# Feed-forward of a transformer layer by Strassen's products of halves, with the hidden activations and the sum in DRAM

## The chip, the cores and the metric

The kernel runs on one core of one Trainium2 chip. The metric is the device time of one execution in microseconds (us); the number that stands for a kernel is the median of several runs. Engines: PE multiplies matrices, DVE (VectorE), ACT (ScalarE) and POOL (GpSimd) work on elements, SP only issues transfers. "PEld" is PE's loading of the stationary operand.

## The reference

One layer of an encoder on x of 512 tokens by 2048 features, in float32: three sub-layers, each `x <- x + RMSNorm(sublayer(RMSNorm(x)))`. The first two (token mixers, cross-attention) are not touched. The third is a dense SwiGLU feed-forward with D_FF = 5632:

```python
def swiglu_ffn(h, w_gu, w_down):
    gate, up = jnp.split(h @ w_gu, 2, axis=-1)     # (512, 2048) @ (2048, 11264)
    return (jax.nn.silu(gate) * up) @ w_down       # (512, 5632) @ (5632, 2048)

x = x + rmsnorm(swiglu_ffn(rmsnorm(x, g[FFN_PRE]), ffn_w_gu[l], ffn_w_down[l]), g[FFN_POST])
```

## The kernel before, in words

Every float32 matrix `a` is split into two float32r tiles, `hi` (ACT casts, L145 or L148) and `lo = a - hi` (DVE, L146 or L149), and a product of two such matrices is three matmuls, hi by hi, hi by lo and lo by hi (`mul3`, L163 to L166). So one instruction of PE takes a stationary block of 128 by 128 and streams 256 or 512 columns past it, and every weight that comes from DRAM costs ACT and DVE one operation each before PE can use it.

Phase 1 (mixers) and phase 2 (cross-attention) run up to about 1403 us. Phase 2 ends with `y_proj`: it leaves y in SBUF, and `advance` (L742 on), for two token tiles of 128 at a time, adds the normed y to the residual stream (L752, in place in the tile `ad_x`), writes that to DRAM (`x2_d`, by a DMA from POOL, L754; the trace calls it `x_d`), transposes it on PE (L218) and splits it into the operand `act`, which is neither normed nor multiplied by the gain: the gain is a scale in the split of the weights (L148, L149), and the norm's factor is multiplied in when the products leave PSUM (`rB`, L928, L931).

Phase 3 is the feed-forward. `gu(b)` makes 512 of the 5632 hidden features by `proj_a`: weights of 128 features by 128 columns are stationary and the tokens stream, 512 columns per matmul; for b = 0 this is done in two halves of 256 tokens, the first of which needs only the first two token tiles. The silu is tanh on ACT (L929) and three operations on DVE (L928 to L931), the product with the up half is L935, and the result is split into `ff_h`, `ff_l` in SBUF. `down(b)` multiplies these 512 features by `proj_b`: the tokens (`ff_h`) are stationary and 512 columns of `w_down` stream; DVE adds the result to y in SBUF (L953). The loop is `gu(0)`, then `gu(b)`, `down(b-1)` for b = 1 to 10, then `last(10)`, which takes one token tile after the other through the last 512 hidden features and the final norm to the output (L981 adds, L983 sums squares, L989 multiplies by the gain, L995 adds the residual).

A scheduler sets each engine's order ahead of time; the engines then run their lists in that order and wait for each other by semaphores. SP issues the loads, in its own order too.

Of the kernel before, what the change touches and what calls it, by code (L numbers as in the profile page):

```python
# [15 lines left out]
P = 128  # L16
# [14 lines left out]
# columns of w_in  # L31
# [4 lines left out]
# columns of the constant tile  # L36
# [3 lines left out]
# columns of the parameter tiles  # L40
# [21 lines left out]
def build(tc, x, mem, norm_g, w_in, conv_a_w, pool_w, pool_scale, gdn_conv_w, gdn_A_log,  # L62
          gdn_dt_bias, gdn_norm_g, ssm_conv_w, ssm_conv_b, ssm_A_log, ssm_dt_bias, ssm_D,
          ssm_norm_g, w_out, xa_wq, xa_wkv, xa_wo, ffn_w_gu, ffn_w_down, cst, out, dbg=None,
# [9 lines left out]
    cp = pool("cp")  # L74
    wp = pool("wp", 3)
    ap_ = pool("actp", 8)
    sm = pool("smp", 4)
    mm = pool("mm", 5, space=PSUM)
    ps = pool("ps", 3, space=PSUM)
# [4 lines left out]
    w_gu, w_down, pool_w = ffn_w_gu[0], ffn_w_down[0], pool_w[0]  # L84
# [9 lines left out]
    r2f = cp.tile([P, NT], F32, name="r2f")  # L94
# [8 lines left out]
    x2_d = dr.tile([T, D], F32, name="x2_d")  # L103
    z_d = dr.tile([T, 512], F32, name="z_d")
# [37 lines left out]
    def split(hi, lo, src, scale=None):  # L142
        """hi + lo = src (times a per-partition scale), each in float32r's bits."""
# [19 lines left out]
    def mul3(o, ah, al, bh, bl, start, stop):  # L163
        nc.tensor.matmul(o, ah, bh, start=start, stop=False)  # L164
        nc.tensor.matmul(o, ah, bl, start=False, stop=False)  # L165
        nc.tensor.matmul(o, al, bh, start=False, stop=stop)  # L166
# [17 lines left out]
    def proj_b(lhs, nk, W, r0, c0, evict, tiles, gain=None, pre=None, done=None):  # L184
        """Token-major: 512 columns of W by the tokens of each tile; lhs(k, t) -> (hi, lo)."""
# [45 lines left out]
    def norm_rows(src, pl):  # L231
        """1 / rms of a token tile [128, 2048], as a column."""
# [37 lines left out]
    def kv_proj(mt, c0, dst, pl, pre=None, done=None):  # L270
        """Keys (or values) of a head, feature-major and split, to DRAM."""
# [60 lines left out]
    def gate_weights(gp):  # L332
        """The sixteen columns of w_in that make the rates, split."""
# [28 lines left out]
    def gates(o, nh, bias, a_log, gp, tg):  # L362
        """Rates and decays of a recurrence's heads, token-major; column nh * t + head."""
# [10 lines left out]
        # softplus(u) = max(u, 0) + log1p(e), e = exp(-|u|); log1p(e) = 2 artanh(e / (2 + e))  # L374
# [662 lines left out]
```

## Time and profile before

| | us |
|---|---|
| median of 3 runs (lowest, highest) | 2879.02 (2877.52, 2879.63) |
| span of the profiled execution, first to last instruction | 2875.84 |
| what lies around the span, median less span | 3.2 |
| phases 1 and 2, to the last matmul of `y_proj` | 1403.5 |
| feed-forward up to the last matmul of `down` | 1416.3 |
| `last(10)`, to the end of the span | 56.0 |

PE is busy for 99% of the span. "Busy" says that a matmul was under way, not that PE went at its peak: the matmuls overlap (a matmul of 512 columns is listed with 0.39 us, the next starts 0.23 us later), so the rate is read from start to start in the timeline, or as a count over a stretch.

### The profile page before, as it was taken

How to read it: one execution, taken by the hardware profiler on the slowest of the kernel's cores; microseconds unless marked ns; L12 is line 12 of the kernel's file. 1: busy time of each engine (PE TensorE's matmuls, PEld its weight loads, DVE VectorE, ACT ScalarE, POOL GpSimd, SP SyncE). 2: the span in 40 equal slices, each digit the busy share in tenths (PEclk: the TensorE clock that was granted, in tenths of full speed). 3: DMA queues.
4: the chain of work that ended last, by engine and by line, in shares of the span. 5: the costliest groups of instructions: out<-in, count | busy, mean ns of one | idle time of the engine just before them, and what ended most of it. 6: DMA issues, size and time to landing. Idle time of an engine off the chain costs nothing.

```text
span 2875.8 us, 34036 instructions
## 1 busy us (share of the span) xinstructions
PE 2836.4 (99%) x13354; PEld 2344.7 (82%) x13354; DVE 1408.4 (49%) x2509; ACT 994.1 (35%) x1648; POOL 84.7 (3%) x135
## 2 busy tenths in 40 slices
PE   8999999999999999999999999999999999999998
PEld 6788788888788878888898888888888888888886
DVE  5736556455842374334963443434444434434446
ACT  5623432333542264334652222222222222222222
POOL 0000000000000010000000000000000000000002
PEclk9999999999999999999999999999999999999999
DMA  8633222344682285424762233233323223332323
GB/s 279 233 103 96 84 74 72 118 132 163 211 319 98 95 311 207 141 88 168 260 195 96 95 96 97 98 99 96 95 95 95 95 95 96 98 98 98 96 98 144
DMA packets 179308, 382.92 MB, mean 133 GB/s; under 512 B 17214, under 2 KB 18123, under 8 KB 173899
## 3 DMA queue, kind: packets, MB, share of 16 engines
q1 hardware_dynamic: 169994, 342.98, 36.4%
q0 software_dynamic: 9152, 37.75, 3.5%
q8 instruction: 105, 1.72, 0.2%
q14 instruction: 57, 0.46, 0.0%
HBM read 338.72 MB, written 41.97 MB: 132 GB/s over the span
## 4 chain that ended last, share of the span: by engine, by line
PE 90%; DVE 4%; issue 2%; DMA 2%; ACT 2%; POOL 0%; SPq 0%; DVEq 0%; ACTq 0%; POOLq 0%
PE mm L164 28%; PE mm L166 28%; PE mm L165 28%; DVE wlo L149 1%; PE ps L520 1%; PE ps L524 1%; DMA raw<-in_xa_wkv_dram 1%; PE ps L218 1%; DVE ad_x L995 0%; DMA memt<-in_mem_dram 0%; ACT gd_jk L430 0%; PE ps L164 0%; ACT whi L148 0%; DVE rsq_t L138 0%; DMA xt<-in_x_dram 0%
## 5 line engine op out<-in xcount | busy, mean ns | idle before, releaser
L149 DVE SCALAR_TENSOR_TENSOR wlo<-raw,PA,whi 128x512 fp32r<-128x512 f32 x752 | 536.2, 747 | 811.2 <-ACT whi L148 807.8
L164 PE MATMUL mm<-act,whi 128*128 128x512 f32 (+1 forms) x2368 | 900.4, 380 | 0.0
L166 PE MATMUL mm<-act,wlo 128*128 128x512 f32 (+1 forms) x2368 | 897.2, 379 | 0.0
L165 PE MATMUL mm<-act,whi 128*128 128x512 f32 (+1 forms) x2368 | 897.1, 379 | 0.0
L148 ACT ACTIVATE whi<-raw,PA 128x512 fp32r<-128x512 f32 x752 | 505.2, 718 | 1023.0 <-PE mm L165 689.8
L166 PEld LDWEIGHTS mm<-act,wlo 128*128 128x128 f32 x2368 | 445.7, 188 | 81.9 <-issue 0.5
L164 PEld LDWEIGHTS mm<-act,whi 128*128 128x128 f32 x2368 | 445.8, 188 | 80.9 <-issue 0.7
L165 PEld LDWEIGHTS mm<-act,whi 128*128 128x128 f32 x2368 | 445.9, 188 | 80.7 <-issue 0.7
L146 DVE TENSOR_TENSOR wlo<-raw,whi 128x1024 fp32r<-128x1024 f32 x172 | 210.5, 1224 | 405.0 <-ACT whi L145 404.8
L145 ACT CAST whi<-raw 128x1024 fp32r<-128x1024 f32 x172 | 180.8, 1052 | 490.7 <-PE mm L166 323.0
L164 PE MATMUL mm<-whi,act 128*128 128x512 f32 x640 | 252.8, 396 | 3.3 <-ACT act L145 3.3
L165 PE MATMUL mm<-wlo,act 128*128 128x512 f32 x640 | 251.9, 394 | 1.8 <-DVE wlo L149 1.8
L164 PE MATMUL mm<-whi,ff_h 128*128 128x512 f32 x640 | 252.6, 395 | 0.0
L166 PE MATMUL mm<-whi,ff_l 128*128 128x512 f32 x640 | 252.5, 395 | 0.0
L165 PE MATMUL mm<-wlo,ff_h 128*128 128x512 f32 x640 | 252.5, 395 | 0.0
L166 PE MATMUL mm<-whi,act 128*128 128x512 f32 x640 | 251.0, 393 | 0.2 <-DVE act L146 0.2
L164 PEld LDWEIGHTS mm<-whi,act 128*128 128x128 f32 x640 | 120.9, 189 | 30.3 <-ACT act L145 5.4
L165 PEld LDWEIGHTS mm<-wlo,act 128*128 128x128 f32 x640 | 121.1, 189 | 27.7 <-DVE wlo L149 3.0
L166 PEld LDWEIGHTS mm<-whi,ff_l 128*128 128x128 f32 x640 | 120.6, 188 | 28.2
L165 PEld LDWEIGHTS mm<-wlo,ff_h 128*128 128x128 f32 x640 | 120.6, 188 | 28.1
L164 PEld LDWEIGHTS mm<-whi,ff_h 128*128 128x128 f32 x640 | 120.6, 188 | 28.1
L166 PEld LDWEIGHTS mm<-whi,act 128*128 128x128 f32 x640 | 121.0, 189 | 25.3 <-DVE act L146 0.6
(363 smaller groups left out, 2179.1 us busy)
## 6 DMA issues: line engine op xcount, KB each, us to landing
raw<-in_ffn_w_gu_dram SPq DMA_DIRECT2D x192, 512.0 KB, 3.4
raw<-in_w_in_dram SPq DMA_DIRECT2D x88, 512.0 KB, 3.5
raw<-in_ffn_w_down_dram SPq DMA_DIRECT2D x88, 512.0 KB, 3.9
raw<-in_xa_wkv_dram SPq DMA_DIRECT2D x64, 512.0 KB, 4.4
raw<-in_w_out_dram SPq DMA_DIRECT2D x32, 512.0 KB, 3.9
raw<-in_xa_wo_dram SPq DMA_DIRECT2D x32, 512.0 KB, 6.2
raw<-in_xa_wq_dram SPq DMA_DIRECT2D x32, 512.0 KB, 4.0
raw<-vw_d SPq DMA_DIRECT2D x28, 512.0 KB, 4.1
```

What stands on the lines that cost most here:

```text
L145: nc.scalar.copy(hi, src)
L146: nc.vector.tensor_tensor(lo, src, hi.bitcast(F32), op=ALU.subtract)
L148: nc.scalar.activation(hi, src, AF.Copy, scale=scale)
L149: nc.vector.scalar_tensor_tensor(lo, src, scale, hi.bitcast(F32), op0=ALU.mult, op1=ALU.subtract)
L164: nc.tensor.matmul(o, ah, bh, start=start, stop=False)
L165: nc.tensor.matmul(o, ah, bl, start=False, stop=False)
L166: nc.tensor.matmul(o, al, bh, start=False, stop=stop)
L218: nc.tensor.transpose(tp[:, j], src[:, k * P:(k + 1) * P], ident)
L520: nc.tensor.matmul(h64(tp)[:, h], A[:, h], Xe[:, h], start=True, stop=True)
L524: nc.tensor.matmul(h64(tp)[:, h], Pm[:, h], half(Y, s, 1)[:, h], start=True, stop=True)
```

## The change

The feed-forward's two products are cut into halves in each of their three dimensions and made by Strassen's scheme (in Winograd's form): seven products of halves where a plain product of halves has eight, for sums and differences of the operands' quarters. Everything else up to the end of phase 2 is left.

- `advance_t` takes the place of `advance` in phase 2: the tile is also normed in place (ACT, after the DMA to `x2_d`), and the transposed tile is multiplied by the gain (DVE) and kept as float32 in `stg`. Only then does `left_parts` (DVE sums, ACT and DVE splits) make the seven left operands, for all 512 tokens.
- `block(j)`, 44 times: gate and up of 128 hidden features. `right_parts` makes the seven right operands from four quarters of the weights (DVE sums L970, L971, L974, L977), each product is 8 x 3 matmuls of 256 columns into one of three PSUM banks, some of them left open and added to by a later product. The result `h` goes to DRAM (`h_d`, by SP).
- `panel(c, n)`, 5 x 2 times: 1024 hidden features by 1024 output columns; a product is 2 x 4 x 3 matmuls of 512 columns. After each product ACT copies two PSUM banks to SBUF (`e`, 4 buffers) and POOL issues a DMA that adds `e` to `y_d` in DRAM (`accum_op`); the first to a place is a plain write. The hidden activations come back from `h_d`, and `left_parts` is run for each of the five chunks.
- `last()`: the last 512 hidden features as before, without Strassen, y read from `y_d`.
- The weights lie in another order in DRAM (`w_gu`, `w_down`, `w_last`), so that each load is 4 or 8 KB in one piece per partition.

```diff
-        gu(0)
-        for b in range(1, NB):
-            gu(b)
-            down(b - 1)
-        last(NB - 1)
+        gate_up(xT)
+        down()
+        last()
```

```diff
+            nc.gpsimd.dma_start(x2_d[rows], xt)
+            n = norm_rows(xt, pl)
+            nc.scalar.activation(xt, xt, AF.Copy, scale=n)
...
+                nc.vector.tensor_tensor(xT[q // 2][t // 2][q % 2][:, :, o:o + P], tp,
+                                        bc(PA[:, 5 * 16 + q * 4:5 * 16 + q * 4 + 4], P), op=ALU.mult)
...
+    ORDER = (1, 2, 6, 5, 7, 3, 4)
...
+    def left_parts(A11, A12, A21, A22, tmp, L):
+        tt = nc.vector.tensor_tensor
+        split3(L[1], A11)
+        split3(L[2], A12)
+        tt(tmp, A21, A22, op=ALU.subtract)
+        split3(L[5], tmp)
+        tt(tmp, tmp, A11, op=ALU.subtract)
+        split3(L[6], tmp)
+        tt(A21, A11, A21, op=ALU.subtract)
+        split3(L[7], A21)
+        tt(A12, A12, tmp, op=ALU.add)
+        split3(L[3], A12)
+        split3(L[4], A22)
...
+    def block(j, L, rp, tp):
...
+        A, B, Cc = (mm.tile([P, 512], F32, name="mm")[:, 0:256] for _ in range(3))
+        bank = {1: A, 2: B, 6: A, 5: Cc, 7: A, 3: Cc, 4: A}
...
+            wh = wp.tile([P, 8, P], F32R, name="whi")
+            wl = wp.tile([P, 8, P], F32R, name="wlo")
+            split3((wh, wl), src)
+            for k in range(8):
+                ah, al = L[m][k // 4]
+                mul3(bank[m], wh[:, k], wl[:, k], ah[:, k % 4], al[:, k % 4],
+                     k == 0 and m in (1, 2, 5), k == 7, True)
...
+        nc.sync.dma_start(h_d[j], h)
...
+    def panel(c, n, L, lb):
...
+            for t in range(2):
+                ts_ = slice(t * P, (t + 1) * P)
+                for k in range(4):
+                    wh, wl = w[k // 2]
+                    mul3(bank[m][t], L[m][0][:, k, ts_], L[m][1][:, k, ts_], wh[:, k % 2], wl[:, k % 2],
+                         k == 0 and m in (1, 2, 5), k == 3, True)
+            for th, fh, sign in to[m]:
+                for t in range(2):
+                    e = lb.tile([P, 512], F32, name="e", bufs=4)
...
+                    if c == 0 and m in first:
+                        nc.gpsimd.dma_start(dst, e)
+                    else:
+                        nc.gpsimd.dma_start(dst, e, accum_op=ALU.add)
```

How the instructions stand on DVE where the feed-forward begins, in the kernel before (its splits of weights and, later, the silu of `gu`):

```order
1404 L149 SCALAR_TENSOR_TENSOR wlo<-raw,PA,whi 128x512 x16
1405 L928 TENSOR_TENSOR ff_g<-mm,rB 128x512 x2
1406 L930 SCALAR_TENSOR_TENSOR ff_g<-ff_t,ff_g 128x512
1407 L928 TENSOR_TENSOR ff_g<-mm,rB 128x512
1408 L931 SCALAR_TENSOR_TENSOR ff_g<-ff_g,rB 128x512
```

and in the changed kernel, from the last token tile's multiplication by the gain (L932) to the second product of the first block (`L1l` to `L7l` are the low parts of the left operands, `f_g` is the gate):

```order
1123 L932 TENSOR_TENSOR stg<-ps,PA 128x4x128 x4
1124 L954 TENSOR_TENSOR stg<-stg 128x1024
1125 L947 TENSOR_TENSOR L1l<-stg,L1h 128x1024
...
1134 L947 TENSOR_TENSOR L1l<-stg,L1h 128x1024
1135 L947 TENSOR_TENSOR L2l<-stg,L2h 128x1024
...
1144 L947 TENSOR_TENSOR L6l<-stg,L6h 128x1024
1145 L947 TENSOR_TENSOR L3l<-stg,L3h 128x1024
1146 L970 TENSOR_TENSOR sum<-raw 128x1024
1147 L1022 TENSOR_TENSOR f_g<-mm,f_x 128x256
1148 L971 TENSOR_TENSOR sum<-sum,raw 128x1024
```

In the place of weights' splits that go with PE there now stand 22 operations on 128 by 1024 elements (rows 1124 to 1145), behind the last tile and ahead of the sums of the first block's weights (L970, L971).

On SP, in the kernel before, the weights of `gu` and `down` follow each other without a break:

```order
174 L153 DMA raw<-in_ffn_w_gu_dram 128x2x512 x16
175 L153 DMA raw<-in_ffn_w_down_dram 128x2x512 x8
176 L153 DMA raw<-in_ffn_w_gu_dram 128x2x512 x16
177 L153 DMA raw<-in_ffn_w_down_dram 128x2x512 x8
178 L153 DMA raw<-in_ffn_w_gu_dram 128x2x512 x16
```

In the changed kernel the chunks of `down` and the end stand like this (`hq` are quarters of the hidden activations, `rawB` the quarters of `w_down`):

```order
262 L1059 DMA hq<-h_d 128x4x256 x3
263 L1070 DMA rawB<-in_w_down_dram 128x2048 x10
264 L1110 DMA raw_24709<-h_d 128x4x512
265 L1117 DMA raw_24715<-in_w_last_dram 128x2048
266 L1122 DMA gB<-in_norm_g_dram 128x2048
267 L1117 DMA raw_24721<-in_w_last_dram 128x2048
268 L1117 DMA raw_24727<-in_w_last_dram 128x2048
269 L1126 DMA ad_x<-x_d 128x2048
270 L1117 DMA raw_24733<-in_w_last_dram 128x2048
271 L1128 DMA y<-y_d 128x2048
```

The loads of the hidden activations and of the last weights stand behind the loads of `down`, and the read of the sum, `y<-y_d`, behind all of them; before, y was never out of SBUF.

## Rows read from the trace of the kernel before

**Rows 1.** The page: busy time of each engine with its share of the span, then the granted clock of PE in 40 slices (tenths of full speed), then the chain of work that ended last, by engine.

```profile
PE 2836.4 (99%) x13354; PEld 2344.7 (82%) x13354; DVE 1408.4 (49%) x2509; ACT 994.1 (35%) x1648; POOL 84.7 (3%) x135
...
PEclk9999999999999999999999999999999999999999
...
PE 90%; DVE 4%; issue 2%; DMA 2%; ACT 2%; POOL 0%; SPq 0%; DVEq 0%; ACTq 0%; POOLq 0%
```

**Rows 2.** Stretches of the span: length, busy time (and count of instructions) of PE, PEld, DVE, ACT and POOL, PE's granted clock, the DMA engines' busy share and GB/s. The whole feed-forward up to `last`, the first half of b = 0, a stretch of `gu` and `down`, then two pieces of the very end.

```profile
1404.00:2820.00 1416.00, 1413.99 (x6568) 1179.03 (x6568) 632.26 (x939) 408.92 (x585) 1.06 (x2) 1.00 0.33 106
...
1404.00:1434.00 30.00, 27.99 (x232) 27.29 (x232) 29.22 (x92) 21.87 (x38) 1.06 (x2) 1.00 0.70 233
...
1434.00:1474.00 40.00, 40.00 (x336) 40.00 (x335) 25.87 (x47) 20.52 (x36) 0.00 (x0) 1.00 0.69 234
...
2865.00:2870.00 5.00, 0.00 (x0) 0.00 (x0) 3.60 (x16) 0.72 (x2) 1.62 (x2) 0.70 0.00 2
2870.00:2876.00 6.00, 0.00 (x0) 0.00 (x0) 2.40 (x4) 0.00 (x0) 0.00 (x0) 0.50 0.46 175
```

**Rows 3.** The timeline of PE, start and duration in us, at four places: `down` (tokens stationary, 512 weight columns streaming), `gu` with 512 tokens streaming, `gu` of b = 0 with 256 tokens streaming, and the first matmuls of the kernel.

```profile
1619.59 0.40 PE L165 MATMUL mm<-wlo,ff_h 128*128 128x512 f32 x1
...
1621.91 0.39 PE L166 MATMUL mm<-whi,ff_l 128*128 128x512 f32 x1
...
1519.79 0.39 PE L166 MATMUL mm<-act,wlo 128*128 128x512 f32 x1
...
1521.15 0.39 PE L166 MATMUL mm<-act,wlo 128*128 128x512 f32 x1
...
1427.57 0.28 PE L166 MATMUL mm<-act,wlo 128*128 128x256 f32 x1
...
1428.76 0.28 PE L164 MATMUL mm<-act,whi 128*128 128x256 f32 x1
...
12.03 0.63 PE L166 MATMUL mm<-whi,act 128*128 128x512 f32 x1
...
12.88 0.63 PE L165 MATMUL mm<-wlo,act 128*128 128x512 f32 x1
```

**Rows 4.** Groups of instructions by line and shape between 1380 us and the end: count, busy time, mean ns of one, then idle time before them and what ended it.

```profile
L164 PE MATMUL mm<-act,whi 128*128 128x512 f32 x1280 | 497.9, 389 | 0.0
L166 PEld LDWEIGHTS mm<-act,wlo 128*128 128x128 f32 x1536 | 289.4, 188 | 50.0
...
L164 PE MATMUL mm<-whi,ff_h 128*128 128x512 f32 x640 | 252.6, 395 | 0.0
...
L146 DVE TENSOR_TENSOR wlo<-raw,whi 128x1024 fp32r<-128x1024 f32 x86 | 105.3, 1224 | 216.9 <-ACT whi L145 216.8
L145 ACT CAST whi<-raw 128x1024 fp32r<-128x1024 f32 x86 | 90.3, 1051 | 310.0 <-PE mm L166 183.4 <-PE mm L165 84.8 <-issue 41.7
L165 PE MATMUL mm<-act,whi 128*128 128x256 f32 x256 | 72.9, 285 | 0.0
...
L930 DVE SCALAR_TENSOR_TENSOR ff_g<-ff_t,ff_g 128x256 f32<-128x256 f32 x8 | 3.1, 419 | 0.0
...
L733 ACT ACTIVATE yjk<-mm 128x512 bf16<-128x512 f32 x5 | 3.0, 593 | 1.3 <-PE mm L166 1.3
```

**Rows 5.** The timeline where phase 2 ends: PE's last matmul of `y_proj` and first of `gu`, then DVE's reduction and residual of one of the last token tiles and of the last one, then ACT's sum of squares.

```profile
1403.47 0.39 PE L166 MATMUL mm<-whi,ptl 128*128 128x512 f32 x1
1403.70 0.28 PE L164 MATMUL mm<-act,whi 128*128 128x256 f32 x1
...
1406.87 0.15 DVE L747 TENSOR_REDUCE rs_s<-yss 128x1 f32<-128x4 f32 x1
...
1410.81 1.41 DVE L752 SCALAR_TENSOR_TENSOR ad_x<-y,rs_r,ad_x 128x512 f32<-128x512 f32 x2
...
1422.32 2.08 DVE L752 SCALAR_TENSOR_TENSOR ad_x<-y,rs_r,ad_x 128x512 f32<-128x512 f32 x3
...
1414.20 1.92 ACT L229 ACTIVATE junk<-ad_x 128x2048 bf16<-128x2048 f32 x1
```

**Rows 6.** DMA issues between 1000 and 1420 us: line engine count, KB of each, median us from issue to landing.

```profile
vw_d<-at_e POOLq DMA_DIRECT2D x32, 256.0 KB, 5.3
x_d<-ad_x POOLq DMA_DIRECT2D x7, 1024.0 KB, 4.9
raw<-in_ffn_w_gu_dram SPq DMA_DIRECT2D x9, 512.0 KB, 4.2
ad_x<-x_d SPq DMA_DIRECT2D x4, 1024.0 KB, 6.5
```

**Rows 7.** Everything that writes or reads `vw_d`, the tile that phase 2 writes to DRAM in pieces of 256 KB, copied from PSUM by ACT into `at_e` (2 buffers) and issued by POOL: durations in ns, first and last start; waits for it; us to landing.

```profile
L877 POOL DMA_DIRECT2D vw_d<-at_e x32: 539/542/547, 1011.0 to 1161.3; - x32
...
  ACT at_e L875: 22.0, 14
...
DMA to landing us min/median/max: 2.8/5.0/8.5
```

**Rows 8.** The chain that ended last, from 2815 us, in order of time: start and length in us. The last columns of the first and of the last token tile, and the end.

```profile
2831.22 0.70 DVE y L981
...
2836.26 3.78 DVE ad_x L995 x4
...
2865.09 0.69 DVE y L981
```

More of the change, by code (lines that the diff above doesn't have):

```diff
@@ L103, in build @@
     x2_d = dr.tile([T, D], F32, name="x2_d")
+    h_d = dr.tile([HT, P, T], F32, name="h_d")
+    y_d = dr.tile([T, D], F32, name="y_d")
     z_d = dr.tile([T, 512], F32, name="z_d")
@@ L894, in phase2 @@
                         value_out(3, pl)
+            es_act.close()
+            stg = pool("stg", 9, "right", es_stg)
             yp = pool("yp2", stack=s0)
             pl2 = pool("adp2", stack=s0)
-            act = [act_quad() for _ in range(4)]
+            xT = [[[stg.tile([P, 4, 256], F32, name="stg") for _ in range(2)] for _ in range(2)] for _ in range(2)]
             def then(i):
-                return lambda y, ss: advance(act, (2 * i, 2 * i + 1), y, ss, x1_d, x2_d, r2f, pl2)
+                return lambda y, ss: advance_t((2 * i, 2 * i + 1), y, ss, xT, pl2)
@@ new lines, in phase2, with advance_t @@
+        return xT, stg
+    def advance_t(tiles, y, ss, xT, pl):
+        for t in tiles:
+            rows = slice(t * P, (t + 1) * P)
+            xt = pl.tile([P, D], F32, name="ad_x", bufs=2)
+            nc.sync.dma_start(xt, x1_d[rows])
+            s = sm.tile([P, 1], F32, name="rs_s")
+            nc.vector.tensor_reduce(s, ss[:, t], axis=AX.X, op=ALU.add)
+            r = sm.tile([P, 1], F32, name="rs_r")
+            mean_rsqrt(r, s, 1, D)
+            for q in range(4):
+                qs = slice(q * 512, (q + 1) * 512)
+                nc.vector.scalar_tensor_tensor(xt[:, qs], y[:, t, qs], r, xt[:, qs], op0=ALU.mult, op1=ALU.add)
+            nc.gpsimd.dma_start(x2_d[rows], xt)
+            n = norm_rows(xt, pl)
+            nc.scalar.activation(xt, xt, AF.Copy, scale=n)
+            for q in range(4):
+                tp = ps.tile([P, 4, P], F32, name="ps")
+                for j in range(4):
+                    k = q * 4 + j
+                    nc.tensor.transpose(tp[:, j], xt[:, k * P:(k + 1) * P], ident)
+                o = t % 2 * P
+                nc.vector.tensor_tensor(xT[q // 2][t // 2][q % 2][:, :, o:o + P], tp,
+                                        bc(PA[:, 5 * 16 + q * 4:5 * 16 + q * 4 + 4], P), op=ALU.mult)
@@ new lines, in right_parts, with gate_up @@
+    def right_parts(B11, B12, B21, B22, new):
+        tt = nc.vector.tensor_tensor
+        yield B11
+        yield B21
+        p, t2 = new(), new()
+        tt(p, B11, B12, op=ALU.add)
+        tt(t2, p, B22, op=ALU.add)
+        yield t2
+        yield p
+        tt(B12, B12, B22, op=ALU.add)
+        yield B12
+        yield B22
+        tt(t2, t2, B21, op=ALU.add)
+        yield t2
+    def gate_up(xT):
+        with ExitStack() as s0:
+            lp = pool("lp", 2, stack=s0, reuse_waits="tile")
+            L = {m: [(lp.tile([P, 4, 256], F32R, name=f"L{m}h"), lp.tile([P, 4, 256], F32R, name=f"L{m}l"))
+                     for _ in range(2)] for m in ORDER}
+            rp = pool("rp", 3, stack=s0, reuse_waits="tile")
+            for sub in range(2):
+                tmp = stg.tile([P, 4, 256], F32, name="stg")
+                left_parts(xT[0][0][sub], xT[1][0][sub], xT[0][1][sub], xT[1][1][sub], tmp,
+                           {m: L[m][sub] for m in ORDER})
+            es_stg.close()
+            tp = pool("tp", 2, "right", s0, reuse_waits="tile")
+            for j in range(HT):
+                block(j, L, rp, tp)
@@ new lines, in build, with down @@
+    NC = HT // 8
+    def down():
+        with ExitStack() as s0:
+            lb = pool("lb", 1, stack=s0, reuse_waits="tile")
+            for c in range(NC):
+                L = {m: tuple(lb.tile([P, 4, 256], F32R, name=f"B{m}" + s) for s in "hl") for m in ORDER}
+                hq = {}
+                for kh in range(2):
+                    for th in range(2):
+                        a = lb.tile([P, 4, 256], F32, name="hq", bufs=5)
+                        k0 = c * 8 + kh * 4
+                        nc.sync.dma_start(a, h_d[k0:k0 + 4, :, th * 256:(th + 1) * 256].rearrange("k p t -> p k t"))
+                        hq[th, kh] = a
+                left_parts(hq[0, 0], hq[0, 1], hq[1, 0], hq[1, 1], lb.tile([P, 4, 256], F32, name="hq", bufs=5), L)
+                for n in range(2):
+                    panel(c, n, L, lb)
@@ L959, in last @@
+    def last():
+        with ExitStack() as s0:
+            pl = pool("lastp", stack=s0, reuse_waits="tile")
+            raw = pl.tile([P, 4, T], F32, name="raw4", bufs=2)
+            nc.sync.dma_start(raw, h_d[HT - 4:HT].rearrange("k p t -> p k t"))
+            hh, hl = (pl.tile([P, 4, T], F32R, name="ff_" + s) for s in "hl")
+            split3((hh, hl), raw)
+            lhs = act_lhs([(hh, hl)])
             ws = []
             for c in range(4):
[L961 to L966 removed]
@@ L973, in last @@
                 nc.sync.dma_start(xt, x2_d[rows])
+                y = pl.tile([P, D], F32, name="y", bufs=2)
+                nc.sync.dma_start(y, y_d[rows])
                 ss = sm.tile([P, 4], F32, name="ff_ss")
@@ L1025 @@
     arrays, args = {}, []
[L1026 to L1027 removed]
+    given = laid_out(inputs)
+    for name in _INS:
+        a = given[name]
         arrays[f"in_{name}_dram"] = a
```

175 lines of the change are left out of this document (97 added, 78 removed).

## The prediction

> **What bounds the kernel now.** I read the page first: PE is busy for 99% of the span, its granted clock is full in every slice, and 90% of the chain that ended last is PE [rows 1]. Then the stretches: in the 1416 us of the feed-forward PE is without a matmul for 2 us, while DVE is busy 632 and ACT 409, and DMA takes a third [rows 2]. So time there goes by how many matmuls PE starts and how far apart. The timeline gives the distances [rows 3]: in `gu` with 512 tokens 1.36 us for 6 (0.2267 each), in `down` 2.32 for 10 (0.232), in the half-width `gu` of b = 0 1.19 for 10 (0.119; the stretch agrees with 336 in 40.00 us [rows 2]). By counts [rows 4]: 3 x 1280 x 0.2267 = 870, 3 x 640 x 0.232 = 445, 3 x 256 x 0.119 = 91, in all 1407 of the 1416. The rest of the reading is what the change needs: what one split costs, what lies between phases, and how DMAs land.
>
> **Gate and up.** 44 blocks x 7 products x 8 x 3 = 7392 matmuls of 256 columns replace 3840 of 512 and 768 of 256. In columns that is exactly 7/8. In time it is less of a gain, because a matmul of 256 does not start twice as often as one of 512: 7392 x 0.1195 = 883 (0.119 by the timeline, 0.12 rounded up; I take the middle) against 961. **-78 us.** Why 256 columns cost 0.119 rather than 0.113 the rows hint at: there PEld is busy 40.00 of 40.00 us [rows 2], so weight loading has nothing to spare, and the change makes all of gate/up such a stretch. The Trainium skill (TensorE: Matmul & The Clock Gate, "Back-to-back issue gap") gives an isolated gap of N/2.4 + 2.5 ns, 109 ns for 256 columns and 216 for 512, and says that it under-counts at small N; by it gate/up would take 806 us, some 77 less than my term. The trace has 119 and 227, and these decide.
>
> DVE and ACT must keep up inside a block of 168 matmuls, 20.1 us of PE. DVE has 7 low parts at 1.224, 4 sums of the same size and about 7 operations of 256 columns at 0.42 [rows 4], 16.4 us; ACT 7 x 1.05 and 5 small ones, 9.4 us. Both have room; I charge nothing for the steady state. The cover is 3.7 us of DVE per block; if DVE took 10% more it would still hold.
>
> **Down.** 10 panels x 7 x 24 = 1680 matmuls of 512, for 1920: 1680 x 0.232 = 390. **-56 us.** A panel is 39 us of PE. DVE has 14 low parts (17.1), 4 sums of 128 x 2048 (twice the 128 x 1024, so 2.4 each: 9.8) and half of a chunk's 11 left operations (6.7): 33.6. ACT has 14 x 1.05 + 14 copies of PSUM at 0.593 [rows 4] + 3.7 = 26.7. DVE fills 86%, and not evenly: a sum of 2.4 and an extra left part may fall into one product of 5.6 us, and the three slots of `whi` allow only a product and a half ahead. I add 1 us for most panels and 2 us at each of the four chunk boundaries, where the fourth left operand can be overwritten only when the last product that reads it is through: **+15 us.** Zero if the slots cover it, 45 if one product in each two loses 1.3 us.
>
> **What now lies bare.** Before, `gu` starts 0.23 us after `y_proj`'s last matmul [rows 5], because b = 0's first half needs only the first two token tiles; the last two are finished beneath it.
>
> (a) Start. Now nothing of the feed-forward can start until all four tiles are through, since the operands are differences of token halves. For the last tiles the reduction starts at 1406.9 and the residual at 1410.8 [rows 5], with splits of weights between; without these I put the residual's start at 1409. It takes 4 x 0.7 for each of two tiles (to about 1415); then come the DMA to `x2_d`, 4.9 [rows 6], which the norming in place has to wait for, the norming, 1.9 (as the sum of squares [rows 5]), and transposes with 4 multiplications by the gain, 0.7 each. Before, the last tile's residual stood at 1422.3 [rows 5] because the weights' splits came in between; those go, but waits on the DMA are new. I take 1430 for the last multiplication (bounds 1424, the chain with no slip, and 1436). Then DVE has 22 operations of 1.2 in the row shown in the order: product 1 can start 12 of them in, product 3 (the sixth operand) only after all and some 7 more for its weights, while PE gets 5.7 us done: the stream is as if it began 26 us after the last multiplication, at 1456. **+52 us** (40 to 65).
>
> (b) Between gate/up and down. SP has the `h` of the last block ahead of the loads of the first chunk: last product's silu and store 1.5, then 4 loads of 512 KB, first landing after 4.2 [rows 6], then 1 MB pieces of weights; then splits and sums for the first three products, some 18 operations of 1.2 on DVE plus three sums of 2.4, of which PE covers two products (11 us). **+23** (15 to 35).
>
> (c) The end. From the last matmul of `down` to the first token tile's fourth addition (2831.2 [rows 8]) 11.4 us passed before, four groups of 12 matmuls. Now the last hidden activations and four weights of 1 MB pass through two buffers, each load about 5 [rows 6], each split 2.1 on ACT and 2.4 on DVE: the fourth weight is split at about +24, the addition at +28. The other three tiles take 11.3 each as before (2831.2 to 2865.1), the tail 10.7: 28 + 34 + 11 = **73 against 56, +17** (8 to 30).
>
> (d) Clock. In the last microseconds, with PE idle, the granted clock reads 0.70, then 0.50 [rows 2], that is 1.2 instead of 2.4 GHz, and the kernel's first matmuls are 0.425 apart instead of 0.23 [rows 3]. Three bare stretches cost one to three us each: **+4** (0 to 9).
>
> **Sum**, against the profiled execution: 1403.7 + 52 + 883 + 23 + 390 + 15 + 73 + 4 = 2844 for 2876, and with the 3.2 that lie around the span about 2847; as terms, -78 - 56 + 52 + 23 + 15 + 17 + 4 = -23, with some -9 for waits of the old stream that the counts left over. I forecast **2848**.
>
> **Accumulating DMAs** are the one thing that the trace doesn't show: 126 of the 140 stores of 256 KB must read and add to DRAM. In a panel products 1 and 2 go to the same place, 5 and 7 too, so the second must wait for the first to land; `e` has four buffers, two per product, and ACT, which also splits the weights, runs in order. Bounds: a plain store of the same size lands in 5.0 (2.8 to 8.5), issue 0.54 on POOL [rows 7], and at two a product (5.6 us) that is hidden, cost 0; the other end is twice that, 10, when each dependent pair would hold ACT about 5 us beyond its slack. From about 8 us per landing it decides. That ACT can be held by such buffers is seen: 22.0 us in 14 waits for `at_e` with two [rows 7]. I take the lower end, since a plain store is the nearest row and DMA is two thirds idle [rows 2].
>
> **Rivals.**
> 1. *Accumulation holds ACT, PE starves* (other side). At 10 us per landing two pairs per panel cost 5 each: 10 panels x 10 = 100, so 2948; at 9 us about 2910. For it: each add reads as well as writes, and the copies are in the same queue as the splits. Against it: 128 descriptors of 2 KB in a DMA system at 0.3. Chance 0.2. The Trainium skill (Collectives: The Full Stack, "The bandwidth ceiling") says that an add in the DMA needs two source reads, and a reduce ran at half the rate of a copy; by that, landings go towards the doubled 10 us if the transfer itself rules the 5.0. No run here shows it yet.
> 2. *Bare stretches and DVE's clumps are dearer*: (a) 65, (b) 35, (c) 30 and 45 within `down` add 68: 2916; halfway there 2882, no change. For it: DVE was busy 29.2 of 30 us in just this stretch at 1404 [rows 2], and every chain there is serial. Chance 0.15.
> 3. *Bare stretches are cheap*: the lower bounds of (a) to (d) and no clumps take 12 + 8 + 9 + 4 + 15 = 48: 2800; a half of it 2824. Chance 0.13.
> 4. *Matmuls of 256 columns are bound by weight loading*: PEld lists 0.188 per load [rows 4]; if that were the distance, 7392 x 0.188 = 1390, some 500 slower. The same row stands beside 0.119 in the timeline, so loads overlap; chance 0.02.
>
> **The numbers.** 0.5 for the forecast, 2835 to 2865 by its own terms. A measurement of this kernel tells about 0.2%, 6 us. Faster takes the forecast, rival 3, and a little of 1 and 2: 0.66; same, halfway in rival 2 or a mild 1: 0.07; slower: 0.27. The range for 8 in 10 runs from 2815, inside rival 3, to 2930, where rival 1 at 9 us and rival 2 still lie.
>
> **What will show it.** In gate/up a count of matmuls by stretch: 8.4 per us if right. From `y_proj`'s last matmul to the first steady block 52 us with PE mostly idle, and DVE on left operands. In `down` 0.232 from start to start with few holes; if rival 1 is right, ACT's copies to `e` wait for `y_d<-e`, whose landings stand near 10, and PE waits for `whi`. If rival 2 is right, PE waits for DVE's low parts with DVE near 100%. The prediction is wrong as a whole if gate/up's matmuls start at other than 0.119, since 0.01 there is 74 us.

## The result, and the profile after

The changed kernel takes 2888.8 us (median of 6 runs, 2883.5 to 2902.6), the kernel before 2878.1 beside it: a ratio of 1.0042 [1.0024, 1.0060], slower by 0.4%. The forecast was 2848, faster by 1.1%, so its sign was wrong; the time itself is inside the range.

The page after, with the lines that answer to [rows 1], then the DMA engines' share in 40 slices and the two large queues (q0 carries the transfers that POOL issues, q1 those that SP issues):

```profile
PE 2751.8 (95%) x15890; PEld 2392.1 (83%) x15890; DVE 1835.1 (64%) x2683; ACT 1259.0 (44%) x1926; POOL 198.6 (7%) x275
...
PEclk9999999999999999999979999999999999999998
DMA  8633222344683276424523333333333338899886
...
q1 hardware_dynamic: 143514, 361.86, 38.3%
q0 software_dynamic: 28288, 74.46, 11.7%
```

PE's busy time fell by 85 us, and PE now stands still for 136 us of the span where it was 39. Two things show in the slices: the clock dips at the start of the feed-forward (a 7), and from the 34th slice on DMA goes from 3 tenths to 8 and 9. That is `down`.

The stretches, cut where the steps of the prediction begin and end (columns as in [rows 2]): the end of `y_proj`; from there until the stream of gate/up runs as if it had never paused; gate/up; the way to `down`'s product with the third operand, the sixth in the order of a panel; the rest of `down`; `last`.

```profile
1406.00:1424.00 18.00, 16.67 (x84) 13.65 (x83) 13.83 (x28) 10.26 (x14) 0.06 (x1) 1.00 0.79 288
1424.00:1476.00 52.00, 18.72 (x82) 17.05 (x80) 43.98 (x92) 23.10 (x23) 1.07 (x2) 0.62 0.10 43
1476.00:2363.00 887.00, 883.92 (x7343) 883.55 (x7344) 685.78 (x788) 386.85 (x524) 0.00 (x0) 1.00 0.36 114
2363.00:2413.40 50.40, 31.57 (x124) 24.34 (x123) 41.15 (x31) 24.81 (x29) 5.07 (x8) 0.83 0.89 309
2413.40:2816.00 402.60, 371.06 (x1561) 299.78 (x1559) 277.24 (x207) 230.43 (x286) 109.82 (x131) 0.97 0.88 191
2816.00:2887.40 71.40, 47.90 (x193) 37.41 (x192) 47.15 (x94) 21.47 (x38) 19.74 (x16) 0.86 0.65 228
```

Against the prediction, step by step (us):

| step | predicted | measured |
|---|---|---|
| last matmul of `y_proj` starts | 1403.7 | 1423.9 |
| (a) start | 52 | 52 |
| gate/up | 883 | 887 (0.1200 from start to start) |
| (b) between, less what PE covers | 23 | 23 (50.4 less 5 products of 5.44) |
| `down`, matmuls | 390 | 381 (1680 x 0.2268) |
| waits within `down` | 15 | 49 (402.6 less 65 products of 5.44) |
| (c) end | 73 | 72 |
| (d) clock | 4 | in the terms above |

Four terms are within 4 us. Three are not: phases 1 and 2, which the change does not touch, take 20 us longer, and `down` waits 34 us more than I allowed, while its matmuls go 9 us faster. +20 + 4 - 9 + 34 - 1 - 4 is +44; the span of 2887.4 misses the sum of 2844 by 43.

**The 20 us in phases 1 and 2.** PE's timeline in the middle of phase 1, before:

```profile
597.74 0.39 PE L165 MATMUL mm<-act,whi 128*128 128x512 f32 x1
...
598.87 0.39 PE L164 MATMUL mm<-act,whi 128*128 128x512 f32 x1
```

and after, five matmuls apart in both:

```profile
597.86 0.40 PE L166 MATMUL mm<-act,whi 128*128 128x512 f32 x1
...
599.03 0.39 PE L168 MATMUL mm<-act,wlo 128*128 128x512 f32 x1
```

The same instructions in the same order are 1.17 us apart where it was 1.13: 0.234 each where [rows 3] have 0.2267. Matched one by one with the kernel before, PE's matmuls lag by 2 us at 490 us, 9 at 835, 19 at 1280 and 20 at the end of `y_proj` (1423.9, [rows 5]: 1403.5), most of it where such matmuls follow each other; they are just further apart. In `down` it is the other way round, 0.2268 where it was 0.232. What did change is where the tiles lie: the change opens its pools in another order and puts `act` on the other side of SBUF.

**The 34 us in `down`.** Transfers between 2400 and 2780 us: queues with packets, MB and share, then issues with count, KB each and median us to landing.

```profile
q0 software_dynamic: 16712, 32.06, 54.2%
q1 hardware_dynamic: 11962, 41.76, 33.6%
...
rawB<-in_w_down_dram SPq DMA_DIRECT2D x33, 1024.0 KB, 7.4
y_d<-e POOLq DMA_DIRECT2D x122, 256.0 KB, 6.1
```

The stores that add move 32 MB and take more of the DMA engines than the 42 MB of loads. What waited between 2365 and 2815 us (us in total, times, longest), on PE, POOL, DVE and ACT, and the one group of matmuls on which most of it falls:

```profile
PE mm L167 <- DVE wlo L947: 32.8, 15, 3.8
POOL y_d L1103 <- DMA y_d<-e: 32.7, 10, 5.5
DVE sumB L971 <- DMA rawB<-in_w_down_dram: 31.5, 9, 4.9
...
ACT e L1095 <- DMA y_d<-e: 4.8, 3, 2.0
...
L167 PE MATMUL mm<-wlo,B7h 128*128 128x512 f32 x73 | 33.3, 457 | 25.4 <-DVE wlo L947 25.4
```

25.4 of PE's 32.8 us stand before `B7h`, the product with the seventh operand, the fifth in the order of a panel: in eight of the ten panels it takes 8.0 to 11.1 us where the other products mostly take 5.44, 37 us more in all. One of these, on DVE and then on PE:

```profile
2490.53 2.29 DVE L971 TENSOR_TENSOR sumB<-sumB,rawB 128x2048 f32<-128x2048 f32 x1 [3.46 <-DMA rawB<-in_w_down_dram]
2492.74 2.28 DVE L974 TENSOR_TENSOR rawB<-rawB 128x2048 f32<-128x2048 f32 x1
2494.94 3.49 DVE L947 TENSOR_TENSOR wlo<-rawB,whi 128x1024 fp32r<-128x1024 f32 x3
...
2496.22 0.80 PE L167 MATMUL mm<-wlo,B7h 128*128 128x512 f32 x1 [3.36 <-DVE wlo L947]
```

DVE's sums for the next panel (L971, L974) stand in its list ahead of low parts of the current one (L947). The load for L971 is issued at 2482.2, when a slot of `rawB` comes free, and lands 8.3 us later; DVE stands 3.46 us with that sum at the head of its list, and PE, which only wants the low part behind it, stands 3.36. ACT's copies to `e`, on which rival 1 rested, waited 4.8 us in all; the stores that must wait for an earlier one to the same place held POOL for 32.7 us, which only issues them.

### The profile page after: what moved, and what is told of

Read it like the earlier page. It is cut to its first block, busy times and chain, and to the rows that moved or that the text cites. A ratio compares the mean times of both kernels' runs of the same rounds, so it can differ in the third digit from the quotient of the medians.

```text
span 2887.4 us, 40226 instructions
## 1 busy us (share of the span) xinstructions
PE 2751.8 (95%) x15890; PEld 2392.1 (83%) x15890; DVE 1835.1 (64%) x2683; ACT 1259.0 (44%) x1926; POOL 198.6 (7%) x275
## 5 line engine op out<-in xcount | busy, mean ns | idle before, releaser
L151 DVE SCALAR_TENSOR_TENSOR wlo<-raw,PA,whi 128x512 fp32r<-128x512 f32 x368 | 263.3, 747 | 313.1 <-ACT whi L150 309.3
L150 ACT ACTIVATE whi<-raw,PA 128x512 fp32r<-128x512 f32 x368 | 248.1, 718 | 415.6 <-PE mm L167 222.6
L166 PE MATMUL mm<-act,whi 128*128 128x512 f32 x832 | 335.0, 403 | 0.0
L168 PE MATMUL mm<-act,wlo 128*128 128x512 f32 x832 | 331.7, 399 | 0.0
L167 PE MATMUL mm<-act,whi 128*128 128x512 f32 x832 | 331.5, 398 | 0.0
L947 DVE TENSOR_TENSOR wlo<-sum,whi 128x1024 fp32r<-128x1024 f32 x132 | 161.3, 1223 | 145.8 <-ACT whi L946 145.8
L148 DVE TENSOR_TENSOR wlo<-raw,whi 128x1024 fp32r<-128x1024 f32 x92 | 112.6, 1225 | 195.5 <-ACT whi L147 195.4
L946 ACT CAST whi<-sum 128x1024 fp32r<-128x1024 f32 x132 | 138.1, 1047 | 215.1 <-PE mm L167 211.1
L947 DVE TENSOR_TENSOR wlo<-raw,whi 128x1024 fp32r<-128x1024 f32 x176 | 215.7, 1225 | 17.5 <-ACT whi L946 13.3
L168 PEld LDWEIGHTS mm<-act,wlo 128*128 128x128 f32 x832 | 156.8, 188 | 36.8 <-issue 0.5
L167 PEld LDWEIGHTS mm<-act,whi 128*128 128x128 f32 x832 | 156.9, 189 | 35.5 <-issue 0.7
L166 PEld LDWEIGHTS mm<-act,whi 128*128 128x128 f32 x832 | 156.9, 189 | 35.5 <-issue 0.7
L1103 POOL DMA_DIRECT2D y_d<-e x124 | 106.9, 870 | 279.1 <-ACT e L1095 142.4
L947 DVE TENSOR_TENSOR wlo<-rawB,whi 128x1024 fp32r<-128x1024 f32 x80 | 96.2, 1220 | 30.8 <-ACT whi L946 30.8
```

Source lines behind the costliest of these rows:

```text
L148: nc.vector.tensor_tensor(lo, src, hi.bitcast(F32), op=ALU.subtract)
L150: nc.scalar.activation(hi, src, AF.Copy, scale=scale)
L151: nc.vector.scalar_tensor_tensor(lo, src, scale, hi.bitcast(F32), op0=ALU.mult, op1=ALU.subtract)
L166: nc.tensor.matmul(o, ah, bh, start=start, stop=False, skip_group_check=reopen)
L167: nc.tensor.matmul(o, ah, bl, start=False, stop=False, skip_group_check=reopen)
L168: nc.tensor.matmul(o, al, bh, start=False, stop=stop, skip_group_check=reopen)
```

## The experiments

**1. Where the tiles lie: sides of SBUF.** The instruction order is the same; the pools lie otherwise.

```diff
-    ap_ = pool("actp", 8, "right", es_act)
+    ap_ = pool("actp", 8, "left", es_act)
...
-            lp = pool("lp", 2, stack=s0, reuse_waits="tile")
+            lp = pool("lp", 2, "right", s0, reuse_waits="tile")
...
-            stg = pool("stg", 9, "right", es_stg)
+            stg = pool("stg", 9, "left", es_stg)
```

(and `tp` to the left, `rp` and the pools of phases 1 and 2 to the right)

> The changed kernel with the operand tiles of phases 1 and 2 (act) back in the lower half of each partition's memory, where they lie in the kernel before, and the other tiles of these phases above; the order of the instructions on every engine is the same as in the changed kernel. Theory P (place): PE starts a matmul of 512 columns 0.227 us after the last where both operands lie low, and 0.233 to 0.235 where one lies high; then phase 2 ends near 1403 instead of 1424 and the time is about 2868. Rival Q: something else of the new program (its size, the chip, DMA traffic) makes phases 1 and 2 slower; then the end of phase 2 stays near 1424 and the time near 2889.

2857.7 us (2853.4 to 2864.0), ratio 0.9926 [0.9911, 0.9941]. `y_proj` ends at 1406.5, 17 us earlier, and the matmuls in phase 1 are 0.227 apart, so 17 of the 20 us are a matter of place. But gate/up went to 0.1173 as well, some 20 us more than the theory of sides had to give.

**2. The same with the kernel before**: only `act` changes its side.

```diff
-    ap_ = pool("actp", 8)
+    ap_ = pool("actp", 8, "right")
```

> The kernel before, with nothing but the operand tiles (act) moved from the lower to the upper part of each partition's memory; same order of instructions. Theory P: gate/up and phases 1 and 2 go from 0.227 to 0.234 per matmul of 512, +26 and +20, while y_proj and down, whose operands move down in turn, go from 0.2325 to 0.227, -13: about 2911. Rival Q: within 5 of 2878.

2879.5 us, ratio 0.9996 [0.9986, 1.0006], and the matmuls with `act` stay 0.227 apart. The theory of sides falls. What goes with the distance in all of these kernels is something else, which the tiles' start addresses in the built programs show: where `act` and `whi` begin at the same address modulo 256 bytes (both 224 before, and here again), the distance is 0.227; where they don't (224 and 64 after), 0.2335 or 0.234. `ff_h` (96) against `whi` (224) before had 0.2325, `whi` and the left operands of `down` after (both 64) have 0.2268.

**3. The map of addresses.** Matmuls alone, for 8 by 8 pairs of start addresses modulo 256, with 512 and with 256 columns; all else of the layer is left out.

```diff
+        S = [cp.tile([P, 264], F32R, name="s" + "abcdefgh"[i]) for i in range(8)]
+        M = [cp.tile([P, 1032], F32R, name="m" + "abcdefgh"[i]) for i in range(8)]
...
+                nc.tensor.matmul(acc, S[a][:, r % 2 * P:r % 2 * P + P], M[b][:, r // 2 % 2 * 512:r // 2 % 2 * 512 + n],
+                                         start=r == 0, stop=r == R - 1)
```

> Matmuls alone, with the rest of the computation left out: eight stationary tiles and eight streaming tiles, each 32 bytes further than the last modulo 256, every pair 36 times with 512 and then with 256 columns; no other engine works meanwhile. Theory M (mod 256), formed after the first four runs: the spacing hangs on whether the two operands' start addresses agree modulo 256. Then for 512 columns the 8 pairs of equal place take 0.227 and the 56 others 0.231 to 0.238, and for 256 columns the 8 take 0.120 and the others 0.117. Rival C (contention): the spacing comes from other engines' or DMA's accesses to the same memory; then all 64 pairs are alike here.

Five pairs, each stretch 35 distances long (matmuls that reach over an edge are counted too). First 512 columns, with the streamed operand's start beyond the stationary one's by 0, 64 and 128 bytes, then 256 columns with 0 and 192:

```profile
309.25:317.20 7.95, 7.95 (x36) 6.58 (x35) 0.00 (x0) 0.00 (x0) 0.00 (x0) 1.00 0.00 0
325.84:333.85 8.01, 8.01 (x36) 6.58 (x35) 0.00 (x0) 0.00 (x0) 0.00 (x0) 1.00 0.00 0
275.63:283.79 8.16, 8.16 (x36) 6.57 (x35) 0.00 (x0) 0.00 (x0) 0.00 (x0) 1.00 0.00 0
695.91:700.09 4.18, 4.18 (x37) 4.18 (x36) 0.00 (x0) 0.00 (x0) 0.00 (x0) 1.00 0.00 0
687.55:691.53 3.98, 3.98 (x37) 3.98 (x36) 0.00 (x0) 0.00 (x0) 0.00 (x0) 1.00 0.02 4
```

Over all 64 pairs, with 512 columns equal starts give 0.227, 64 bytes 0.229, every other difference 0.233 to 0.234. With 256 columns equal starts are among the slowest, 0.1195 (a difference of 96 has the same), and the best is a streamed operand that starts 192 bytes beyond the stationary one (or 64 short of it): 0.1137 in the row above, 0.113 to 0.114 in seven of the eight such pairs and 0.118 in one. DVE, ACT and POOL stand idle here and DMA is at 0.02 at most, so rival C falls; theory M holds for equal starts and had missed that the other differences are not alike. The 0.12 of gate/up was thus not owed to the number of columns alone.

**4. Only the addresses.** 160 bytes of padding ahead of `act` and of the left operands; then 192 ahead of the second, for the 0.113. Order as in the changed kernel.

```diff
+    pool("pad", 1, "right", es_act).tile([P, 40], F32, name="pad")
     ap_ = pool("actp", 8, "right", es_act)
...
+            pool("pad2", 1, stack=s0).tile([P, 40], F32, name="pad2")
             lp = pool("lp", 2, stack=s0, reuse_waits="tile")
```

> The changed kernel with two unused pads of 160 bytes, one ahead of the operand tiles of phases 1 and 2 (act), so that they start at the same place modulo 256 as the split weights, one ahead of the left operands of gate/up, so that these do not; nothing else moves, the order of the instructions is the same. Theory M: phase 2 ends near 1405 instead of 1424 (-19) and gate/up's matmuls start 0.117 apart instead of 0.120 (-20): 2848 to 2854. Rival C or P (high and low): phase 2 still ends at 1424, about 2889.

> As the changed kernel with the two pads, but with 192 bytes instead of 160 ahead of gate/up's left operands, so that they start 64 bytes short of the split weights modulo 256; the run of matmuls alone had 0.113 us at that distance for 256 columns, 0.117 at the other and 0.120 at none. Theory M: gate/up starts its matmuls 0.113 to 0.114 apart, 7392 x 0.004 = 29 us less than with 160 bytes: 2825 to 2832. Rival: DVE (16.4 us of a block's 19) or the loads hold gate/up now, 2840 to 2857.

The first: 2856.6 us (2849.2 to 2861.2), 0.9919 [0.9898, 0.9940]. `y_proj` ends at 1402.7, 21 us earlier; gate/up goes at 0.1173. The second: 2821.7 (2818.3 to 2854.2; three of the four runs lie under 2823), 0.9829 [0.9775, 0.9883]. A stretch of 760 us of gate/up, with 160 bytes and then with 192:

```profile
1510.00:2270.00 760.00, 760.00 (x6480) 760.00 (x6479) 600.67 (x696) 341.58 (x462) 0.00 (x0) 1.00 0.38 121
```

```profile
1510.00:2270.00 760.00, 760.00 (x6709) 760.00 (x6708) 616.44 (x720) 354.22 (x480) 0.00 (x0) 1.00 0.39 124
```

PE is listed as busy all the time in both, as in the changed kernel's own gate/up above, but the matmuls start 0.1173 and 0.1133 us apart where it had 0.1200: 160 bytes are worth 20 us in gate/up and 32 more make it 49. With 160 bytes the first product of `down` starts 41 us earlier (2337.1 for 2378.0); 4 of these were lost again in `down`.

**5. The same for the kernel before**, so that the two are compared alike: 128 bytes ahead of the pools of `pth` and `ff_h`.

```diff
-            pp = pool("ptp", stack=s0)
+            pool("padp", stack=s0).tile([P, 32], F32, name="padp"); pp = pool("ptp", stack=s0)
...
-        pl = pool("ffp")
+        pool("padf").tile([P, 32], F32, name="padf"); pl = pool("ffp")
```

> The kernel before with two unused pads of 128 bytes, ahead of the hidden activations of down and of the softmax operands of y_proj, so that these start at the same place modulo 256 as the split weights; order of instructions unchanged. Theory M: 2112 matmuls of down and last and 384 of y_proj go from 0.2325 to 0.227: -13, 2864 to 2869. Otherwise within 4 of 2879.

2863.8 us (2862.9 to 2867.0), 0.9949 [0.9933, 0.9966]; `y_proj` and `down` go at 0.227. So the two algorithms are fairly compared only with the layout repaired in both.

**6. Plain stores in `down`.** Every store to `y_d` is a plain write: the adding is left out, the bytes are the same.

```diff
-                    if c == 0 and m in first:
+                    if True:
                         nc.gpsimd.dma_start(dst, e)
```

> The changed kernel with all 140 stores of the partial sums to DRAM as plain writes: the adding up is left out. Theory S (slots): in down PE waits since the fourth quarter of the next panel's weights is issued only when a slot of six comes free, so this changes little: 2878 to 2889, and the seventh product still takes 9 us or more. Rival A (adding): the adding DMAs fill the DMA engines and make the loads land late (8 us for 1 MB); then the loads land in 5 us, the seventh product takes 5.5 to 7 us and the time is 2855 to 2865.

2858.8 us (2857.4 to 2861.0), 0.9931 [0.9914, 0.9947]: 30 less than the changed kernel, and all of it in `down`, from the first product to the last 406 us for 438 (`y_proj` still ends at 1424.6). POOL's queue and the landings as above:

```profile
q0 software_dynamic: 10631, 34.87, 23.8%
...
y_d<-e POOLq DMA_DIRECT2D x133, 256.0 KB, 3.7
rawB<-in_w_down_dram SPq DMA_DIRECT2D x33, 1024.0 KB, 5.8
```

and the waits, in the same stretch as above:

```profile
POOL y_d L1101 <- DMA y_d<-e: 37.0, 13, 4.9
...
PE mm L167 <- DVE wlo L947: 12.9, 14, 1.9
DVE sumB L971 <- DMA rawB<-in_w_down_dram: 11.8, 8, 2.1
```

Without the adding q0's share falls from 54.2% to 23.8% for rather more bytes, the weights land in 5.8 for 7.4 us, and the waits of PE and of DVE shrink to about 40%. POOL waits for earlier stores to the same place as long as before (37.0 us for 32.7), so that order between stores is not where the 30 us lie. Worked out from the q0 rows over 380 us and 16 engines: with adding 0.542 x 380 x 16 / 16712 = 197 ns for a packet of 1.9 KB, without 0.238 x 380 x 16 / 10631 = 136 ns for one of 3.3 KB, so 103 ns and 41 ns per KB.

**7. One more slot.** Seven buffers of `rawB` for six; the room comes from `e`, whose place a pair of tiles in `wp` takes.

```diff
-                b = lb.tile([P, 4, 512], F32, name="rawB", bufs=6)
+                b = lb.tile([P, 4, 512], F32, name="rawB", bufs=7)
...
+                    e2 = wp.tile([P, 2, 512], F32, name="raw")
```

> The changed kernel with seven slots instead of six for the quarters of the down weights (the copies of PSUM take the place of tiles that lie unused in down), adding DMAs kept. Theory S: the fourth quarter is issued some 10 us earlier, the seventh product goes from 10 us towards 5.5, nine times 4.5 and a few us of slow clock less: 2845 to 2860. Rival A: the loads land later still for DMA is full, DVE still waits for them, 2880 to 2890. Rival D: DVE's two sums ahead of the splits are the stall, whatever the loads do: about half remains, 2870.

2884.9 us (2878.2 to 2888.3), 1.0019 [1.0009, 1.0028]: almost nothing; `down` takes 431 us for 438. The seventh operand's product is at 5.44 us in every panel behind the first, so the late slot was what held it; but the wait moved to the next thing that comes by DMA:

```profile
PE mm L167 <- DVE wlo L947: 32.1, 9, 9.1
...
DVE hq L954 <- DMA hq<-h_d: 27.8, 3, 10.2
```

PE waits as long as before, in 9 pieces for 15. Now the hidden activations of three of the later chunks come late (`hq` lands after 14.5 us), and a product at the chunk's start takes 15.8.

**8. Half of the adding stores.** POOL adds two results in SBUF first, so that 64 adding stores are left of 124.

```diff
+                    if m != 4:
+                        h = held[th, fh, t]
+                        nc.gpsimd.tensor_tensor(h, h, e, op=ALU.add)
+                        e = h
```

> The changed kernel with partial sums for the same place of the output added up in pairs by POOL before they are stored: 80 stores of 256 KB instead of 140, 64 of them adding instead of 124. Theory A (adding fills the DMA engines): their busy share in down falls from 0.88 to about 0.65, DVE's waits for weights from 31 us to 10 or less, product 7 goes to about 6 us: 2860 to 2870. Rival B: POOL's adds on SBUF slow DVE or come too late, and PE waits as before: 2880 to 2895.

> Both of the last two edits together. If the two causes are independent the gains add up: 2889 - 38 - 25 = about 2826, faster than the kernel before by 1.8%. If a faster gate/up or a busier POOL brings DVE or DMA to its limit: 2835 to 2850.

2912.8 us (2906.4 to 2915.1), 1.0109 [1.0092, 1.0127]: slower by 24 than the changed kernel and beyond what either theory had, though DMA's share in `down` (2400 to 2700 us) fell from 0.90 to 0.64, as theory A asked, and the wait of L971 from 31.5 to 20.7 us, where it asked for 10. POOL and DVE in that kernel between 2400 and 2800 us (columns as in [rows 4]):

```profile
L1104 POOL TENSOR_TENSOR e<-e,raw 128x512 f32<-128x512 f32 x53 | 91.5, 1726 | 214.7 <-ACT raw L1098 139.0 <-ACT raw L1096 75.6
L947 DVE TENSOR_TENSOR wlo<-rawB,whi 128x1024 fp32r<-128x1024 f32 x69 | 88.8, 1308 | 17.4 <-ACT whi L946 17.3
...
L977 DVE TENSOR_TENSOR sumB<-sumB,rawB 128x2048 f32<-128x2048 f32 x9 | 27.8, 3085 | 0.1
```

and in the changed kernel:

```profile
L947 DVE TENSOR_TENSOR wlo<-rawB,whi 128x1024 fp32r<-128x1024 f32 x74 | 89.0, 1220 | 27.8 <-ACT whi L946 27.8
L977 DVE TENSOR_TENSOR sumB<-sumB,rawB 128x2048 f32<-128x2048 f32 x10 | 22.9, 2288 | 0.2
```

The same low parts take 1308 ns in place of 1220, and the sums L977 3085 in place of 2288: DVE is slowed while POOL adds. Of the ten sums L977 in `down`, three ran beside no addition and took 2287 ns, seven were overlapped by one for over 0.3 us and took 3453. PE waits 42.8 us for low parts where it waited 32.8. The Trainium skill (SBUF — State Buffer, "two separate sides") has the rule: a VectorE instruction with two operands in SBUF and a GpSimd one that reads SBUF use one pair of ports, one at a time. The rows agree with it. Here the 60 additions on POOL (53 in the stretch above, 1.7 us each) cost more than the 60 adding stores they saved: `down` takes 457 us for 438. With the 160 bytes of experiment 4 as well: 2871.6 (2863.6 to 2880.9), 0.9973 [0.9958, 0.9989], where the two effects added up give 2881: the padding helps here as it did alone, within what such a kernel varies.

**9. All of it without POOL's additions**: the padding of 160 and 192 bytes, seven slots, and the hidden activations loaded a panel ahead and issued by ACT, so that they don't stand behind `rawB` on SP. Then the same with plain stores (the adding left out).

```diff
-                        nc.sync.dma_start(a, h_d[k0:k0 + 4, :, th * 256:(th + 1) * 256].rearrange("k p t -> p k t"))
+                        nc.scalar.dma_start(a, h_d[k0:k0 + 4, :, th * 256:(th + 1) * 256].rearrange("k p t -> p k t"))
...
+                panel(c, 0, L, lb)
+                if c + 1 < NC:
+                    hq = quarters(c + 1)
+                panel(c, 1, L, lb)
```

> The pads (160 and 192 bytes), seven slots for the quarters of the down weights, and the loads of the hidden activations for the next chunk asked for a panel earlier and issued by ACT instead of SP, so that they no longer stand behind loads that wait for a slot; adding DMAs kept. With seven slots alone product 7 no longer waited, but product 2 of each new chunk waited 10 us for the hidden activations. If lateness of the loads is the whole of the stall in down, both waits go, down takes 400 to 415 instead of 438 and the time is 2795 to 2810. If the adding DMAs' share of the DMA engines sets the pace whatever the order, down stays above 425: 2815 to 2830.

> The last kernel (pads, seven slots, hidden activations loaded early by ACT) with all stores of partial sums as plain writes; the adding up is left out. If the adding DMAs are what is left of the stalls in down, PE's waits for low parts there fall from 22 us to 6 or less, product 6 takes 5.5 instead of 9 to 12, down 398 to 408 instead of 428, the time 2790 to 2798. If DVE's load or the loads' own pace is what is left: 2810 or more.

2816.3 us (2815.5 to 2819.6), 0.9788 [0.9773, 0.9802]: the lowest median of the kernels that compute the layer, 1.7% below the padded kernel before; the 5 us to padding alone (2821.7) are within that kernel's interval. `down` takes 428 us from first to last product, 9 or 10 less than with the padding alone, but it starts 9 us later (2318.8 for 2310.1): the first chunk's `hq` now come beside SP's seven loads of weights and no longer ahead of them, and the operations on them wait 21.2 us for their landing where they waited 8.3 with the padding alone (2270 to 2345 us). A later chunk's start no longer waits. What does:

```profile
PE mm L167 <- DVE wlo L947: 20.5, 10, 3.7
...
DVE rawB L974 <- DMA rawB<-in_w_down_dram: 21.7, 7, 4.9
...
2400.00:2700.00 300.00, 279.52 (x1176) 224.84 (x1175) 220.73 (x164) 177.96 (x220) 84.32 (x99) 0.97 0.94 205
```

and with plain stores:

```profile
PE mm L167 <- DVE wlo L947: 3.6, 6, 1.2
...
DVE rawB L974 <- DMA rawB<-in_w_down_dram: 5.5, 4, 2.4
...
2400.00:2700.00 300.00, 296.24 (x1288) 239.78 (x1287) 234.41 (x174) 192.69 (x239) 57.99 (x107) 1.00 0.62 215
```

With the adding, DMA is at 0.94 and the wait sits on the weights again, one sum further on; without it `down` takes 402.6 us (one run, 2796.0), DMA 0.62, and DVE and PE hardly wait. Both came out where their expectations had put the adding DMAs as the cause. So the adding stores cost `down` 32 us with six slots and still 25 with seven and early loads.

## Why the prediction was wrong, step by step

- **The span before the change** was taken over: the sum begins with 1403.7 because phases 1 and 2 keep their instructions and their order. Unspoken in that is that a matmul takes what it took. It did not: +20 us, and padding alone takes them back (experiment 4). No view of the trace before could have warned of this by itself, but two rows could have been asked why they differ: `gu` at 0.2267 and `down` at 0.232 for the same 512 columns [rows 3].
- **"Accumulating DMAs: I take the lower end"** is the step that failed most: cost 0, by the row of a plain store and by a DMA that is two thirds idle [rows 2, 7]. Replacing them by plain stores is worth 30 us. The waits within `down` were 49 for 15, and with plain stores they are 17 by the same count (`down` ends 32 us earlier): the 15 held for what it was worked out from, and the term put at 0 measured some 32. (There are 124 such stores and not 126: 16 of the 140 are the first to their place.) The idle share was read in the kernel before, and was the cover that the change itself took away: 54.2 + 33.6% of the engines' time were gone in `down`.
- **Rival 1 had the cause and not the way.** It has `e` hold ACT from about 8 us per landing on. The adding stores landed in 6.1, and ACT waited 4.8 us; the dependent pairs held POOL instead, and did so with plain stores too (experiment 6). The price came by the loads: weights at 7.4 us instead of 5.8, a sum of the next panel at the head of DVE's list, PE behind it. The landing of the stores themselves was the wrong thing to watch; what their packets take from everyone else's transfers was the right one.
- **Of the 49 us**, PE is without a matmul for 31.5 (402.6 less 371.1). Some 11 more are the clock: 53 matmuls in that stretch start 0.43 apart, 0.2 more than the rest and as far as the kernel's first ones [rows 3], and the granted clock there is 0.97. In experiment 6, with no wait for low parts above 1.9 us, it reads 1.00 between 2400 and 2700 us. I had set 4 us for the clock in the whole kernel, in the bare stretches alone.
- **Matmuls of `down`, 390 for 381**: 0.232 was the cadence of a layout in which `ff_h` and `whi` start apart; the new one starts them alike. The error helped by 9.
- **Gate/up, 883 for 887**: the term held, and for a reason that I gave wrongly. I ascribed 0.119 to weight loading, because PEld is busy all the time [rows 2]. It is busy all the time at 0.1133 as well (experiment 4). The figure held because the operands of gate/up start alike modulo 256 (both 64), as those of b = 0 did before (both 224), and equal starts have 0.1195 in experiment 3 too; that was luck, since nothing in the prediction asked for it. My sentence against it, that 0.01 there is 74 us, shows what lay in it: 49 us, to be had for 192 bytes of padding.
- **The Trainium skill's 109 ns for 256 columns** (TensorE: Matmul & The Clock Gate, "Back-to-back issue gap") was set aside for the rows' 119. The lowest distance that a run showed, 0.1133, lies nearer to it; the trace's 0.12 is right for this layout only.
- **Start 52, between 23, end 73** came out at 52, 23 and 72. They were worked out along the chains from durations, with the order of DVE counted row by row; here this held. Of the 23, though, I had counted to the third product in order; measured are 15 us ahead of the first product and 8 within the first five, so that it agrees in size more than in place. Rivals 2, 3 and 4 did not come about.

What stays open: why a difference of start addresses costs what it does, and why 256 columns like another one than 512; and how much of the adding stores' price is the adding and how much their smaller packets (1.9 KB against 3.3). Neither was tried. Nor do the rows say why the wait of L971 fell no further than to 20.7 us with half of the adding stores (experiment 8).

## What to carry to other kernels

When a change moves pools about, look up where the stationary and the streamed operand of each matmul begin, modulo 256 bytes, before and after: the matmuls of untouched code may change by 3%, and a padding of a few dozen words repairs it. Price a new kind of DMA by what it takes from the engines' time beside the other transfers of that stage, not by its own landing, and read idle shares with the change's own traffic added. Where an engine's list holds the next stage's sums ahead of the current stage's operands, one late load stops both; one more buffer, in experiment 7, mostly moved the wait to the next transfer.

## What the runs showed of the hardware that I had not expected

- The distance of float32r matmuls depends on the start addresses of both operands: for 512 columns 0.227 (equal modulo 256 bytes), 0.229 (64 further) or 0.233 to 0.234; for 256 columns from 0.1133 to 0.120, with equal starts among the slowest. PE is listed as busy throughout in all of these.
- Stores that add in DRAM took 103 ns of a DMA engine per KB, plain ones 41: in 380 us 54.2% of all engines' time for 32 MB where it was 23.8% for 35. The packets differ too, 1.9 and 3.3 KB.
- POOL's additions of 128 by 512 lengthened DVE's operations on two tiles in SBUF, by 7% (128 by 1024) and 35% (128 by 2048) in the groups shown.
